# Handing out the next weights' four parts one product at a time, and queueing their VectorE work behind the last addition, in a Winograd-style TensorE trunk

## The chip, the cores and the metric

The kernel runs on one core of a Trainium2 chip. The metric is the device time of one launch in microseconds; three runs of the kernel before gave a median of 2574.48 us (2574.34 to 2576.41).

## The reference

The reference is one layer of a streaming encoder on 2048 tokens of width 1024, in float32. Cut to what matters here:

```python
h = rmsnorm(x, norm_mix_w)
u_b, u_c, u_h, z, xbc, dt_raw = jnp.split(h @ w_in, SPLITS, axis=-1)      # 1024 -> 5648
y_a = u_b * causal_dwconv(u_c * u_h, short_conv_w)                        # group A
y_b = ssd_mixer(z, xbc, dt_raw, ...)                                      # group B: chunked scan
x = x + concat([y_a, y_b]) @ w_out                                        # 2048 -> 1024
h = rmsnorm(x, norm_mlp_w)
x = x + square(relu(h @ w_up)) @ w_down                                   # 1024 -> 4096 -> 1024
return rmsnorm(x, final_norm_w)
```

So the work is four large products (w_in, w_out, w_up, w_down) with a state-space scan between the first two.

## The kernel before

**Products.** Every float32 operand is cut into a rounded part `hi` and the remainder `lo`, and a product is three matmuls: hi·hi, hi·lo, lo·hi (lines 300 to 302). Most products also go through a seven-product scheme for 2x2 blocks (class `Seven`): instead of eight block products, seven are made from sums of the blocks, called `b11 t1 t2 b21 t3 b22 t4`, in this order. One run of the seven is a **chain**; `chain` (line 273) writes it. A product of a chain is 12 matmuls of 128x512 (6 in one short chain). There are 113 chains: 20 and 22 for w_in (first and second half of the tokens), 8 for the first half of w_out ("outs"), 16 and 16 for w_up, 31 for w_down ("down"). The second half of w_out is made by plain products (`Output.unit`), between 1134 and 1328 us.

**Accumulators.** A chain uses three PSUM tiles, x, y and w. `b11`, `t2`, `t3` and `t4` all accumulate on x: x is read after t2, again after t3, and again after t4, and TensorE may not go on writing into it before the reader is done. So t4 needs the reader of t3, which has the time of one product (b22) for it, and t3 needs the reader of t2, with b21 between. `t1` and `b22` accumulate on y, `b21` on w.

**Evictions.** After each product `evict` reads the accumulator. In the w_in chains (`Proj.pair`, line 897) and the w_up chains (`Mlp.pair`, line 1143) t1 and t2 are copied by ScalarE, and t3 and b22 are added by VectorE (`add`, lines 928 and 1152). In the outs chains (`out_pair`, line 990, addition in line 1005) and the down chains (`Mlp.down`, line 1310, addition in line 1353) VectorE adds after all of the last six products.

**Weights.** The next chain's weights come as two raw tiles r0 and r1 (tag `wraw`, three buffers), loaded on SyncE's queue. `combine` (line 255) makes four parts of them, and each part is cut into `whi` (ScalarE, line 113) and `wlo` (VectorE, line 114), four buffers each:

```python
yield split_w(r0, nc.vector)                      # part 1, for b11 and b21
... s12 = r1a + r1b (L260);  s12b = s12a - r0a    # part 2, for t1 and t2
yield split_w(s12, nc.vector)
... s34a = r0a - r1a;  s34b = r0b - s12b          # part 3, for t3 and b22
yield split_w(s34, nc.vector)
yield split_w(r1[:, b], nc.vector)                # part 4, for t4
```

Here a and b are the two halves of a tile; `sub` is line 237, so L237 is any subtraction of this kind, on weights or on other blocks. Where the second half of the tokens meets the same w_in columns again, and in the later down chains, s12 and s34 are read back from DRAM (stored by lines 263 and 269), and VectorE has only the `wlo` part. The sums were computed 80 times.

**What sets the order.** The program is traced in this order: seven products, after each the evictions, then the parts that are handed out there (lines 314 to 318), then `after(name)`, which carries the side work (loading and cutting of the next blocks, the scan, the norms). A scheduler then fixes one queue for each engine. It takes an instruction as soon as it believes its inputs and buffers are ready; the order of the trace only decides between instructions that are ready together. So the sums of a later chain's weights can stand in VectorE's queue well ahead of an addition of an earlier chain. The queues themselves are strictly in order at run time: an instruction that waits holds up all that stand behind it. `behind(ins)` (line 108) adds an edge without a semaphore: whatever instruction in the block runs on the engine of `ins` is queued behind `ins`. Instructions on other engines are not touched by it.

In `chain`, `self.evicted` is the last ScalarE copy of t1 or t2 in a `Proj.pair`; in `Mlp` it is never set and the edge is empty. `self.added` is set in line 1353 alone, and used in `finish_first` (line 1497).

Of the kernel before, what the change touches and what calls it, by code (L numbers as in the profile page):

```python
# [14 lines left out]
ALU = mybir.AluOpType  # L15
# [24 lines left out]
def trunk(ctx: ExitStack, tc: tile.TileContext, x, x_tok, w_in, w_dt, w_out, w_up, w_down, cvec, hrow, out):  # L40
    nc = tc.nc
# [44 lines left out]
        out=tri, in_=tri, compare_op=ALU.is_ge, fill=0.0, base=0, pattern=[[1, P]], channel_multiplier=-1  # L86
# [21 lines left out]
    def behind(before):  # L108
        return tc.issue_after(before) if before is not None else nullcontext()
# [22 lines left out]
    def take(it, n=None):  # L132

        return list(itertools.islice((w for w in it if w is not None), n))
# [6 lines left out]
    def psum(tag, name, bufs=1):  # L141
        if tag in turns:
            tag, bufs = next(turns[tag])
        return ps.tile([P, 512], F32, tag=tag, name=name, bufs=bufs)

    class Rstd:


        def __init__(self, pool, tmp, n, w):
            self.pool, self.tmp, self.scale, self.w, self.n = pool, tmp, 1.0 / n, w, w // P  # L150
# [66 lines left out]
    class Seven:  # L217
        def __init__(self):
            self.places = [{} for _ in range(4)]
            self.unsettled = self.evicted = None  # L220
            self.amid = None

        def raw(self, name):
# [49 lines left out]
        def chain(self, groups, ws, ahead, evict, after):  # L273

            n = sum(len(g) for g in groups)
            pm = [{} for _ in groups]
            got = []
            PRODUCTS = (
                ("b11", 0, 0, "x", 1),
                ("t1", 1, 0, "y", 1),  # L280
                ("t2", 1, 1, "x", 0),
                ("b21", 0, 1, "w", 0),
                ("t3", 2, 0, "x", 0),
                ("b22", 2, 1, "y", 0),
                ("t4", 3, 0, "x", 0),
            )
            for name, wn, half, acc, first in PRODUCTS:
                at = half * n
                for gi, g in enumerate(groups):
                    if first:  # L290
                        pm[gi][acc] = psum("mm", "p" + acc, accs["mm"])
                    p = pm[gi][acc]
                    i, j = WHERE[name]
                    for k, place in enumerate(g):
                        if k == 2 and self.amid is not None:
                            self.amid()
                        hi, lo = (t[:, (at + k) * P : (at + k + 1) * P] for t in ws[wn])
                        h = [t[:, j] for t in place[i]]
                        kw = dict(skip_group_check=not first)
                        nc.tensor.matmul(p, hi, h[0], start=bool(first and k == 0), stop=False, **kw)  # L300
                        nc.tensor.matmul(p, hi, h[1], start=False, stop=False, **kw)  # L301
                        nc.tensor.matmul(p, lo, h[0], start=False, stop=(k == len(g) - 1), **kw)  # L302
                    at += len(g)
                for gi in range(len(groups)):
                    if name == "b11":

                        pm[gi]["w"] = psum("mw", "pw", accs["mw"])
                        self.copied = nc.scalar.copy(pm[gi]["w"], pm[gi]["x"]).ins  # L308
                    else:
                        evict(name, gi, pm[gi])  # L310
                if name == "b11" and self.unsettled:
                    self.settle(*self.unsettled, self.copied)
                    self.unsettled = None
                if ahead is not None:
                    if name == "t1":
                        next(ahead)
                    with behind(self.evicted):
                        got += take(ahead, {"b21": 2, "b22": 1, "t4": 1}.get(name, 0))
                after(name)
            return got  # L320

# [146 lines left out]
    class Proj(Seven):  # L468
# [428 lines left out]
        def pair(self, h, what, ws, ahead, after):  # L897
# [15 lines left out]
            else:  # L913
                a, b = self.e("ea"), self.e("eb")
            offb = 2 if kind == "ch" else off
            to = {
                "c11": a[:, off : off + TB],
                "c12": a[:, off + TB : off + TH],
                "c21": b[:, offb : offb + TB],
                "c22": b[:, offb + TB : offb + TH],  # L920
            }
            s = {}
# [3 lines left out]
                self.evicted = nc.scalar.copy(s[name], pm).ins  # L926

            def add(o, pm, name):
                nc.vector.tensor_tensor(out=to[o], in0=pm, in1=s[name], op=ALU.add)

            def evict(name, gi, pm):
                if name == "t1":
# [3 lines left out]
                elif name == "b21":  # L936
# [4 lines left out]
                    else:  # L941
                        nc.scalar.copy(to["c11"], pm["w"])
                elif name == "t3":
                    add("c22", pm["x"], "s5")
                    if kind == "z":
                        silu(to["c22"], to["c22"])
                    elif kind == "b":
                        mul(to["c22"], to["c22"], self.cc[n + 4][:, hi])
                elif name == "b22":
                    add("c12", pm["y"], "s2")  # L950
                    if kind == "z":
                        silu(to["c12"], to["c12"])
# [37 lines left out]
        def out_pair(self, n, ws, ahead, after):  # L990
            b0, b1 = (self.res.pop((n, b)) for b in range(NBB))
            lo, hi = slice(0, TB), slice(TB, TH)
            to = {"c11": (b0[:, lo], 0, 0), "c21": (b0[:, hi], 0, 1), "c12": (b1[:, lo], 1, 0), "c22": (b1[:, hi], 1, 1)}

            def evict(name, gi, pm):
                c, p, fin = {
                    "t1": ("c22", "y", 0),
                    "t2": ("c12", "x", 0),
                    "b21": ("c11", "w", 1),
                    "t3": ("c22", "x", 1),  # L1000
                    "b22": ("c12", "y", 1),
                    "t4": ("c21", "x", 1),
                }[name]
                t, b, i = to[c]
                nc.vector.tensor_tensor(out=t, in0=pm[p], in1=t, op=ALU.add)
                if fin:
                    nc.sync.dma_start(x1_d[n // 4 * NBB + b][:, 2 * (n % 4) + i], t)

            return self.chain([self.places], ws, ahead, evict, after)
# [115 lines left out]
    class Mlp(Seven):  # L1125
# [17 lines left out]
        def pair(self, h, q, ws, ahead, after):  # L1143

            e0, e1, e2 = (self.wide(n) for n in ("e0", "e1", "e2"))
            s = {}

            def copy(pm, name):
                s[name] = self.tmp(name)
                nc.scalar.copy(s[name], pm)  # L1150

            def add(o, pm, name):
                nc.vector.tensor_tensor(out=o, in0=pm, in1=s[name], op=ALU.add)

            def relu2(o, i):
                nc.scalar.activation(o, i, AF.Relu)
                nc.scalar.activation(o, o, AF.Square)

            def evict(name, gi, pm):
                if name == "t1":  # L1160
                    copy(pm["y"], "s5")
                elif name == "t2":
                    copy(pm["x"], "s2")
                elif name == "b21":
                    relu2(e0[:, 0], pm["w"])
                elif name == "t3":
                    add(e2[:, 1], pm["x"], "s5")
                    relu2(e2[:, 1], e2[:, 1])
                elif name == "b22":
                    add(e0[:, 1], pm["y"], "s2")  # L1170
                    relu2(e0[:, 1], e0[:, 1])
                else:
                    relu2(e1[:, 1], pm["x"])

            got = self.chain([self.places], ws, ahead, evict, after)
            self.unstored = h, q, e0, e1, e2
            return got
# [738 lines left out]
    with ExitStack() as c1:  # L1916
# [56 lines left out]
        for n in range(16, 32):  # L1973
# [4 lines left out]
            if n == 30:  # L1978
                ahead = mlp.weights(mlp.load_cols(w_up, (0, 1)))
# [78 lines left out]
```

## Time and profile before

| | |
|---|---|
| median of 3 runs | 2574.48 us (2574.34 to 2576.41) |
| the profiled execution's own time | 2574.36 us |
| its span, first to last instruction | 2572.5 us |
| TensorE matmul busy | 2556.2 us (99%), 11940 matmuls |
| VectorE busy | 1934.1 us (75%) |
| ScalarE busy | 1392.1 us (54%) |
| DMA | 546.44 MB, mean 212 GB/s |

All numbers of a profile come from one execution. Between the span and its own time lie 1.86 us outside the first and last instruction. A matmul's recorded end is modelled and overlaps the next one's start, so a stall of TensorE is read in two ways: as the idle time given in brackets before an instruction, and as the distance of two starts.

### The profile page before, as it was taken

How to read it: one execution, taken by the hardware profiler on the slowest of the kernel's cores; microseconds unless marked ns; L12 is line 12 of the kernel's file. 1: busy time of each engine (PE TensorE's matmuls, PEld its weight loads, DVE VectorE, ACT ScalarE, POOL GpSimd, SP SyncE). 2: the span in 40 equal slices, each digit the busy share in tenths (PEclk: the TensorE clock that was granted, in tenths of full speed). 3: DMA queues.
4: the chain of work that ended last, by engine and by line, in shares of the span. 5: the costliest groups of instructions: out<-in, count | busy, mean ns of one | idle time of the engine just before them, and what ended most of it. 6: DMA issues, size and time to landing. Idle time of an engine off the chain costs nothing.

```text
span 2572.5 us, 33309 instructions
## 1 busy us (share of the span) xinstructions
PE 2556.2 (99%) x11940; PEld 2103.7 (82%) x11940; DVE 1934.1 (75%) x2611; ACT 1392.1 (54%) x2158; POOL 69.4 (3%) x97
## 2 busy tenths in 40 slices
PE   9999999999999999999999999999999999999999
PEld 7887888888888887888888888888888888888887
DVE  7787686778887889978866865755559877876875
ACT  6553345876567865555345555655556444444443
POOL 1011000000000100000000000000000000000001
PEclk9999999999999999999999999999999999999999
DMA  6666455656556678878755764644358766676872
GB/s 232 225 215 243 155 166 192 200 188 205 187 176 193 188 238 284 301 256 266 246 186 200 277 219 160 243 161 154 139 176 273 256 200 208 222 241 216 280 253 78
DMA packets 266165, 546.44 MB, mean 212 GB/s; under 512 B 24848, under 2 KB 108432, under 8 KB 266000
## 3 DMA queue, kind: packets, MB, share of 16 engines
q1 hardware_dynamic: 265568, 543.92, 62.9%
q8 instruction: 94, 1.54, 0.2%
q14 instruction: 71, 0.58, 0.1%
q10 hardware_dynamic: 432, 0.39, 0.0%
HBM read 361.25 MB, written 182.98 MB: 212 GB/s over the span
## 4 chain that ended last, share of the span: by engine, by line
PE 91%; DMA 3%; ACT 2%; DVE 2%; issue 1%; SPq 0%; DVEq 0%; ACTq 0%
PE px L300 15%; PE px L301 15%; PE px L302 15%; PE py L300 7%; PE py L301 7%; PE py L302 7%; PE pw L300 4%; PE pw L302 4%; PE pw L301 4%; PE pm L137 3%; PE pm L139 3%; PE pm L138 3%; PE pm L524 1%; DMA ul<-y_d 1%; PE yd L1678 1%; DMA wraw<-w_down 1%
## 5 line engine op out<-in xcount | busy, mean ns | idle before, releaser
L300 PE MATMUL px<-uh,whi 128*128 128x512 f32 x1800 | 705.3, 392 | 5.0 <-DVE acc L1353 2.2
L301 PE MATMUL px<-ul,whi 128*128 128x512 f32 x1800 | 700.9, 389 | 0.8 <-DVE ul L369 0.6
L302 PE MATMUL px<-uh,wlo 128*128 128x512 f32 x1800 | 700.7, 390 | 0.0
L300 PEld LDWEIGHTS px<-uh,whi 128*128 128x128 f32 x1800 | 338.0, 188 | 81.0 <-DVE acc L1353 5.0
L302 PEld LDWEIGHTS px<-uh,wlo 128*128 128x128 f32 x1800 | 337.9, 188 | 71.4 <-DVE wlo L114 0.5
L301 PEld LDWEIGHTS px<-ul,whi 128*128 128x128 f32 x1800 | 338.0, 188 | 70.1 <-DVE ul L369 1.6
L113 ACT CAST whi<-s 128x1024 fp32r<-128x1024 f32 (+1 forms) x222 | 232.5, 1047 | 288.8 <-PE py L301 146.4
L114 DVE TENSOR_TENSOR wlo<-wraw,whi 128x1024 fp32r<-128x1024 f32 (+1 forms) x224 | 222.3, 992 | 182.6 <-ACT whi L113 182.2
L300 PE MATMUL py<-uh,whi 128*128 128x512 f32 x900 | 355.5, 395 | 0.0
L301 PE MATMUL py<-ul,whi 128*128 128x512 f32 x900 | 351.1, 390 | 0.0
L302 PE MATMUL py<-uh,wlo 128*128 128x512 f32 x900 | 351.0, 390 | 0.0
L114 DVE TENSOR_TENSOR wlo<-s,whi 128x1024 fp32r<-128x1024 f32 (+1 forms) x222 | 269.9, 1216 | 73.3 <-ACT whi L113 72.3
L113 ACT CAST whi<-wraw 128x1024 fp32r<-128x1024 f32 (+1 forms) x224 | 194.3, 867 | 235.4 <-PE px L301 169.7
L300 PEld LDWEIGHTS py<-uh,whi 128*128 128x128 f32 x900 | 169.0, 188 | 39.6 <-issue 4.8
L302 PEld LDWEIGHTS py<-uh,wlo 128*128 128x128 f32 x900 | 169.0, 188 | 35.4 <-issue 0.2
L301 PEld LDWEIGHTS py<-ul,whi 128*128 128x128 f32 x900 | 169.1, 188 | 33.9 <-issue 0.5
L356 DVE TENSOR_TENSOR ul<-rh,uh 128x1024 fp32r<-128x1024 f32 (+1 forms) x128 | 138.7, 1086 | 51.5 <-ACT uh L355 51.1
L300 PE MATMUL pw<-uh,whi 128*128 128x512 f32 x450 | 175.6, 390 | 0.0
L301 PE MATMUL pw<-ul,whi 128*128 128x512 f32 x450 | 175.2, 389 | 0.0
L302 PE MATMUL pw<-uh,wlo 128*128 128x512 f32 x450 | 175.1, 389 | 0.0
L355 ACT CAST uh<-rh 128x1024 fp32r<-128x1024 f32 (+1 forms) x128 | 119.9, 944 | 96.8 <-PE py L302 57.7
L308 ACT COPY pw<-px 128x512 f32<-128x512 f32 x118 | 67.6, 573 | 105.7 <-PE px L302 105.4
(266 smaller groups left out, 3612.9 us busy)
## 6 DMA issues: line engine op xcount, KB each, us to landing
hid_d<-e SPq DMA_DIRECT2D x96, 512.0 KB, 4.1
rh<-hid_d SPq DMA_DIRECT2D x96, 512.0 KB, 4.6
wraw<-w_in SPq DMA_DIRECT2D x67, 512.0 KB, 4.4
wraw<-w_up SPq DMA_DIRECT2D x62, 512.0 KB, 4.3
wraw<-w_down SPq DMA_DIRECT2D x88, 256.0 KB, 4.3
dec<-rd_d SPq DMA_DIRECT2D x32, 512.0 KB, 5.4
wraw<-w_out SPq DMA_DIRECT2D x32, 512.0 KB, 5.1
x<-x SPq DMA_DIRECT2D x24, 512.0 KB, 5.6
```

The costliest lines, as they stand in the source:

```text
L113: nc.scalar.copy(hi, raw)
L114: eng.tensor_tensor(out=lo, in0=raw, in1=hi.bitcast(F32), op=ALU.subtract)
L137: nc.tensor.matmul(out, whi, hi, start=(k == 0), stop=False)
L138: nc.tensor.matmul(out, whi, lo, start=False, stop=False)
L139: nc.tensor.matmul(out, wlo, hi, start=False, stop=(k == nk - 1))
L300: nc.tensor.matmul(p, hi, h[0], start=bool(first and k == 0), stop=False, **kw)
L301: nc.tensor.matmul(p, hi, h[1], start=False, stop=False, **kw)
L302: nc.tensor.matmul(p, lo, h[0], start=False, stop=(k == len(g) - 1), **kw)
L308: self.copied = nc.scalar.copy(pm[gi]["w"], pm[gi]["x"]).ins
L355: nc.scalar.copy(p[i][0], t)
L356: nc.vector.tensor_tensor(out=p[i][1], in0=t, in1=p[i][0].bitcast(F32), op=ALU.subtract)
L524: last[engine] = make(*args, **kw).ins
```

## The change

The four parts are handed out one each after b21, t3, b22 and t4, where before two came after b21 and one each after b22 and t4. And what a part issues on VectorE is queued behind the last addition that the evictions made (`self.added`), which three more lines now record.

```diff
     class Seven:
         def __init__(self):
             self.places = [{} for _ in range(4)]
-            self.unsettled = self.evicted = None
+            self.unsettled = self.evicted = self.added = None
             self.amid = None
...
                 if ahead is not None:
                     if name == "t1":
                         next(ahead)
-                    with behind(self.evicted):
-                        got += take(ahead, {"b21": 2, "b22": 1, "t4": 1}.get(name, 0))
+                    with behind(self.evicted), behind(self.added):
+                        got += take(ahead, name in ("b21", "t3", "b22", "t4"))
                 after(name)
...
             def add(o, pm, name):
-                nc.vector.tensor_tensor(out=to[o], in0=pm, in1=s[name], op=ALU.add)
+                self.added = nc.vector.tensor_tensor(out=to[o], in0=pm, in1=s[name], op=ALU.add).ins
...
                 t, b, i = to[c]
-                nc.vector.tensor_tensor(out=t, in0=pm[p], in1=t, op=ALU.add)
+                self.added = nc.vector.tensor_tensor(out=t, in0=pm[p], in1=t, op=ALU.add).ins
...
             def add(o, pm, name):
-                nc.vector.tensor_tensor(out=o, in0=pm, in1=s[name], op=ALU.add)
+                self.added = nc.vector.tensor_tensor(out=o, in0=pm, in1=s[name], op=ALU.add).ins
```

`name in (...)` is True or False and counts as one part or none. The three hunks at the end are lines 929 (`Proj.pair`), 1005 (`out_pair`) and 1153 (`Mlp.pair`); line 1353 set `self.added` already.

## Rows read from the trace of the kernel before

**Rows 1.** The page: busy time of each engine.
```profile
PE 2556.2 (99%) x11940; PEld 2103.7 (82%) x11940; DVE 1934.1 (75%) x2611; ACT 1392.1 (54%) x2158; POOL 69.4 (3%) x97
```

**Rows 2.** Stretches (outs, w_up, down): us; PE, PEld, DVE, ACT, POOL busy; clock; DMA.
```profile
955.00:1134.00 179.00, 175.85 (x878) 143.30 (x877) 158.62 (x226) 102.87 (x178) 0.00 (x0) 1.00 0.80 272
1653.00:1977.00 324.00, 324.00 (x1431) 268.39 (x1430) 200.17 (x264) 178.27 (x266) 0.00 (x0) 1.00 0.51 179
1977.00:2525.00 548.00, 545.73 (x2400) 449.52 (x2400) 423.67 (x528) 239.26 (x277) 0.00 (x0) 1.00 0.69 228
```

**Rows 3.** Waits of TensorE's matmuls, whole span: us in total, times, longest.
```profile
PE px L300 <- DVE acc L1353: 2.2, 4, 0.9
PE pss L1713 <- DVE ssq L1707: 1.9, 3, 0.7
PE px L300 <- ACT uh L368: 1.2, 1, 1.2
PE px L300 <- DVE x L1005: 1.2, 2, 0.8
```

**Rows 4.** Timeline (start, us), TensorE, a down chain: b22's last matmul, t4's first.
```profile
2041.10 0.39 PE L302 MATMUL py<-uh,wlo 128*128 128x512 f32 x1
2042.38 0.50 PE L300 MATMUL px<-uh,whi 128*128 128x512 f32 x1 [0.89 <-DVE acc L1353]
```

**Rows 5.** Timeline of VectorE, same chain; L1353 px is t3's addition.
```profile
2037.38 1.22 DVE L114 TENSOR_TENSOR wlo<-s,whi 128x1024 fp32r<-128x1024 f32 x1
2041.03 0.69 DVE L260 TENSOR_TENSOR s<-wraw 128x512 f32<-128x512 f32 x1 [2.44 <-DMA wraw<-w_down]
2041.64 0.68 DVE L1353 TENSOR_TENSOR acc<-px,acc 128x512 f32<-128x512 f32 x1
2042.24 0.68 DVE L237 TENSOR_TENSOR s<-s,wraw 128x512 f32<-128x512 f32 x1
```

**Rows 6.** Timeline of SyncE's queue, same chain: when the late load was issued.
```profile
2035.75 0.81 SPq L1227 DMA_DIRECT2D wraw<-w_down  x2
```

**Rows 7.** Timeline of VectorE at the other three such places.
```profile
2061.11 0.69 DVE L260 TENSOR_TENSOR s<-wraw 128x512 f32<-128x512 f32 x1 [2.55 <-DMA wraw<-w_down]
...
2118.82 0.69 DVE L260 TENSOR_TENSOR s<-wraw 128x512 f32<-128x512 f32 x1 [2.11 <-DMA wraw<-w_down]
...
2176.68 0.69 DVE L260 TENSOR_TENSOR s<-wraw 128x512 f32<-128x512 f32 x1 [2.14 <-DMA wraw<-w_down]
```

**Rows 8.** Timeline, an outs chain; L1005 px is t3's addition, the matmul t4's first.
```profile
1039.67 1.21 DVE L114 TENSOR_TENSOR wlo<-s,whi 128x1024 fp32r<-128x1024 f32 x1
...
1041.93 0.68 DVE L1005 TENSOR_TENSOR x<-px,x 128x512 f32<-128x512 f32 x1
...
1042.67 0.50 PE L300 MATMUL px<-uh,whi 128*128 128x512 f32 x1 [0.33 <-DVE x L1005]
```

**Rows 9.** Timeline of VectorE, just ahead of the other addition L1005 waited for.
```profile
974.71 1.89 DVE L369 TENSOR_TENSOR ul<-ul,uh 128x512 fp32r<-128x512 f32 x3
```

**Rows 10.** ScalarE by line and shape, 1977 to 2525 us: count, busy, mean ns, idle.
```profile
L113 ACT CAST whi<-s 128x1024 fp32r<-128x1024 f32 x56 | 59.0, 1053 | 35.1 <-PE py L301 15.6 <-PE pw L301 14.3 <-DVE s L237 2.2
```

**Rows 11.** Timeline, outs: part 2's wlo of the next chain, t1's first use of it.
```profile
982.50 1.23 DVE L114 TENSOR_TENSOR wlo<-s,whi 128x1024 fp32r<-128x1024 f32 x1
...
984.51 0.40 PE L302 MATMUL py<-uh,wlo 128*128 128x512 f32 x1
```

**Rows 12.** Timeline at one of the scan's waits.
```profile
821.78 1.22 DVE L114 TENSOR_TENSOR wlo<-s,whi 128x1024 fp32r<-128x1024 f32 x1
...
824.27 0.35 PE L1713 MATMUL pss<-ssq,ones_r 128*128 128x128 f32 x1 [0.72 <-DVE ssq L1707]
```

**Rows 13.** Timeline, a w_up chain: a load of r1, t3's addition, the load's sum.
```profile
1453.72 0.33 SPq L105 DMA_DIRECT2D wraw<-w_up  x1
...
1457.05 0.69 DVE L1153 TENSOR_TENSOR e<-px,s 128x512 f32<-128x512 f32 x1 [0.63 <-PE px L302]
1458.44 0.69 DVE L260 TENSOR_TENSOR s<-wraw 128x512 f32<-128x512 f32 x1 [0.71 <-DMA wraw<-w_up]
```

## The prediction

> **What bounds the kernel now.** I read the page's busy line first [rows 1]: TensorE's matmuls cover 99% of the span, while VectorE has 75% and ScalarE 54%. A matmul's end is modelled, so I took the busy time by stretch next [rows 2], to see what a full TensorE looks like. From 1653 to 1977 us it is never idle and starts 1431 matmuls in 324.00 us, one every 0.226 us, at clock 1.00. So 12 matmuls, one product of a chain, take 2.72 us, and a chain of seven 19.0 us. The down stage has 548.00 − 545.73 = 2.3 us without a matmul, the outs 179.00 − 175.85 = 3.2 us. That is about all that a better order can win there: the kernel runs at TensorE's pace, and this change removes no matmul. The third view, TensorE's waits [rows 3], names what can go: 2.2 us for the addition of line 1353 and 1.2 us for that of line 1005. The other two lines, the scan's ssq and the cut of fresh blocks in line 368, are touched only indirectly.
>
> The timeline then says why the additions are late. In a down chain b22 issues its last matmul at 2041.10, and t4's first comes at 2042.38 [rows 4]. In between, VectorE runs L260, the first sum of part 2, then t3's addition, then the next sum [rows 5]. L260 had sat 2.44 us at the head of the queue, waiting for a load of raw weights, and the addition behind it had been ready since about 2038.6, when t3's product ended (one product, 2.72 us, ahead of b22's end). The load it stood behind was issued at 2035.75 and used at 2041.03 [rows 5, 6]. These are not the weights of the next chain, whose part 2 gets its wlo at 2037.38, but of the one after it: the scheduler expected the load earlier and placed the sum a chain ahead of its place in the program's trace. The same pattern, with 2.55, 2.11 and 2.14 us at L260, stands three more times [rows 7], and those are the four waits for L1353.
>
> **The change part by part.** It adds and removes no instruction and no transfer. It moves four things.
>
> *Part 2 goes from b21 to t3, and its VectorE work behind t3's addition.* L260 of those four places goes behind the addition of the following chain, 19 us later, when its load has long landed, and the sum that is now due in this chain stands behind this chain's addition. So no sum stands ahead of it. t3's addition starts when its product ends and takes 0.68 us, and t4 has 2.72 us of b22 as cover. So the wait goes. Its worth is more than the idle time: from 2041.10 to 2042.38 are 1.28 us where 0.226 would do, so 1.05 us is lost for 0.89 us idle, 0.16 more. For four waits that is 2.2 [rows 3] + 4 x 0.16 = 2.84 us. In the outs, t4 waited 0.33 us for t3's addition at 1041.93, and part 2's wlo, 1.21 us, stood ahead of it [rows 8]. With it behind, the addition comes 1.1 us sooner, which ends this wait too: 0.33 + 0.16 = 0.49 us. The other wait for L1005, 0.8 us, I leave as it is: ahead of that addition stand three cuts of fresh blocks, 1.89 us [rows 9], and no weights. Sum: −3.33 us.
>
> *What part 2 loses.* From t3's end its chain is: addition 0.68, L260 0.69, L237 0.68 [rows 5], whi on ScalarE 1.05 [rows 10], wlo 1.23 [rows 11], together 4.3 us. t1 of the next chain uses wlo after b22, t4 and b11 (8.15 us) and two matmuls (0.45), so 4.3 us are left for other work in VectorE's queue. Below, this costs nothing, since nothing in it can speed TensorE up; above, it costs 2.72 us in a chain, if part 2 comes one whole product later than before where it had nothing to spare. The nearest row is the outs chain where 0.78 us was to spare (982.50 + 1.23 to 984.51 [rows 11]). There the sum stood behind t3's addition already, so I take nothing, and keep 2.72 − 0.78 = 1.9 us for the range.
>
> *Parts 1, 3 and 4.* Part 1's wlo is queued behind b21's own addition in outs and down, one instruction of 0.68 us. It is needed by b11, three products (8.15 us) later: nothing. In w_in and w_up the last addition at b21 is that of the chain before, so the edge binds nothing. Parts 3 and 4 wait for the additions of b22 and t4, but t3 and t4 of the next chain use them five and six products later: nothing. What is queued behind a waiting addition on VectorE is the side work and the scan; both ends of its cost are with the rivals. ScalarE's instructions get no new edge, but part 2's whi now waits for the later sums, and what stands behind it waits too: the last evictions of the chain and cuts of blocks, none of which TensorE needs before part 2 itself, in the next chain. Nothing again.
>
> *Transfers.* r0's buffer is held until s34b, and that is now behind b22's addition. In w_up the next r1 is issued at 1453.72 and its sum runs at 1458.44, 4.7 us later [rows 13]. After the change r0 comes free about 2.72 + 0.68 + 2 x 0.68 = 4.8 us after t3's addition started at 1457.05, at 1461.8, so the load lands near 1466.5. Its sum is not due until behind the next chain's t3 addition, at 1457.05 + 19.0 + 0.7 = 1476.8. The cover is 10 us. On SyncE's queue the stores of s12 and s34 (lines 263 and 269) come later with their sums and may hold the loads behind them; those feed blocks and weights due a product or more later. I cost both at nothing; if the cover were gone, one late block costs what the row of line 368 shows, 1.2 us [rows 3].
>
> So the profiled execution's 2574.36 us less 3.33 gives **2571.0 us**. That execution lies 0.12 us below the median of 2574.48, so it needs no shift: −0.13%.
>
> **The rivals.** *Buffers, not order (0.20).* The late sums come from a load that waits for one of three raw buffers: the four waits at L260 are alike, 2.1 to 2.6 us, and the load is issued only 5.3 us ahead [rows 5 to 7]. The change adds no buffer and holds r0's longer. If the additions are held up again, by the cut of other blocks or by b22-side sums, the gain is gone: 2574.4 us, no change. Against it: t3's addition needs no buffer of that load, only its place in the queue. The Trainium skill (Perfetto Trace Analysis, section Optimization Strategy) says that the same gap repeated on an engine can mean that there is no room for the next tile to be allocated, so that buffer counts or tile sizes are what to look at. By that rule alone the gap would outlive a change of order; the four alike waits fit it, but no row shows the addition itself short of a buffer.
>
> *More than the additions (0.17).* In the scan stage TensorE waits three times, 1.9 us, for ssq [rows 3], and at 824.27 a weights' wlo of 1.22 us stands in VectorE's queue shortly ahead of it [rows 12]. If the parts, spread out, no longer bunch there, 1.9 + 3 x 0.16 = 2.4 us go as well: 2571.0 − 2.4 = 2568.6. Against it: the scan's work is placed by the scheduler, and nothing ties it to the additions.
>
> *Part 2 late at t1 (0.12).* This is the case on the other side. In the outs VectorE is busy 158.62 of 179.00 us, 89% [rows 2], so the 4.3 us to spare shrink to little, and every instruction that the scheduler now puts between t3's addition and part 2's wlo counts. Each chain in which it comes a product later with only 0.78 us in hand waits 1.9 us; eight outs chains make 15.5 us: 2586.5. It decides the sign from 3.3 us of such waits on, and makes the kernel slower by over 0.2% from 8.5 us on, 1.06 us in each of eight chains. Against it: VectorE is at 77% in down (423.67 of 548.00) and 62% in w_up (200.17 of 324.00), so there it has room.
>
> **How the numbers follow.** 0.2% of 2574.48 is 5.15 us, about what a measurement of this kernel can tell from no change. My forecast has 0.51; around it I allow 0.05 beyond −5.15 us, if small waits go too, and 0.02 beyond +5.15. Faster: 0.05 + 0.17 = 0.22. Slower: 0.12 + 0.02 = 0.14. The same: 0.64. The range starts at 2567.6, a microsecond under the second rival, takes in the forecast and the first rival, and ends at 2577.5, which holds the forecast with three waits of 1.9 us lost; beyond lie most of the third rival and a thin tail below.
>
> **What would show it.** Right: L260 stands behind t3's addition in every down chain, no matmul waits for L1353, DMA waits of L260 shrink or go since the loads land a chain ahead, and part 2's wlo still ends before t1. TensorE's busy time by stretch changes by 2 to 3 us in down and 0.5 us in the outs, elsewhere not at all. Wrong: matmuls that wait for wlo (L114) at t1, new waits of pss for ssq, or t3's additions held up by other work.

## The result and the profile after

The changed kernel takes 2590.47 us (median of 6 runs, 2586.17 to 2594.23) against 2574.93 us (6 runs beside it): a ratio of 1.0059, 95% interval 1.0049 to 1.0069. It is slower by 15.5 us, 0.6%, where 2571.0 us had been forecast. The profiled execution took 2591.25 us with a span of 2589.5.

Page of the changed kernel, busy line:

```profile
PE 2563.8 (99%) x11940; PEld 2105.1 (81%) x11940; DVE 1927.0 (74%) x2611; ACT 1385.3 (53%) x2154; POOL 73.5 (3%) x97
```

Against [rows 1], VectorE and ScalarE are busy for 7 us less and TensorE's modelled busy time is up by 8. VectorE and TensorE have the same instructions and ScalarE four table loads fewer (the loads of tables for its activations); they stand in another order. The next two fences are stretches (us; PE, PEld, DVE, ACT, POOL busy; clock; DMA). The first is of the kernel before, for the second half of w_in beside the scan. The second is of the changed kernel: the same chains, from the start of the first to the start of the outs, then two stretches as long as those of [rows 2] for the outs and down, begun 15 and 16 us later:

```profile
452.00:955.00 503.00, 500.76 (x2598) 411.98 (x2597) 403.76 (x565) 352.66 (x654) 20.07 (x39) 1.00 0.62 196
```

```profile
452.40:966.10 513.70, 507.04 (x2599) 414.13 (x2598) 399.12 (x564) 347.26 (x649) 22.19 (x38) 1.00 0.61 192
970.00:1149.00 179.00, 174.19 (x867) 141.46 (x867) 157.40 (x226) 100.92 (x176) 0.00 (x0) 1.00 0.80 268
1993.00:2541.00 548.00, 545.58 (x2400) 449.78 (x2400) 426.83 (x533) 236.88 (x277) 0.00 (x0) 1.00 0.69 230
```

The same matmuls beside the scan, to within one, take 513.70 us instead of 503.00. The outs start 11 matmuls fewer in 179 us, and down as many as in [rows 2]. The clock is 1.00 in all of these. Laying the starts of the 113 chains (numbered from 0; chains 20 to 41 are those beside the scan) of the two traces side by side says the same: the changed kernel is 0.4 us late when the scan begins, 10.8 us when the outs begin, 15.1 at w_up, 16.9 at down and 16.7 at the end. Four chains of down come sooner, by 1.20, 1.03, 0.59 and 0.65 us: 3.47 together; others of down give as much back. What TensorE's matmuls now wait for (us in total, times, longest):

```profile
PE px L300 <- ACT pw L308: 6.0, 6, 1.5
PE px L300 <- DVE x L1005: 2.5, 4, 1.0
PE py L300 <- ACT s L1150: 1.7, 1, 1.7
PE st L138 <- DVE xde L1624: 1.5, 4, 0.6
...
PE px L300 <- DVE acc L1353: 0.8, 1, 0.8
PE yd L1678 <- DVE dec L1659: 0.8, 1, 0.8
...
PE py L302 <- DVE wlo L114: 0.4, 1, 0.4
```

Of [rows 3], the wait for ssq is gone, and L1353 falls from four waits to one, elsewhere. At the head is a ScalarE copy that had one wait of 0.3 us before, in w_up: L308 copies b11's accumulator, which t2 goes on writing. The place of [rows 4, 5] now looks as planned. VectorE, then TensorE, of the changed kernel:

```profile
2057.22 0.69 DVE L1353 TENSOR_TENSOR acc<-px,acc 128x512 f32<-128x512 f32 x1 [0.63 <-PE px L302]
2057.82 0.68 DVE L260 TENSOR_TENSOR s<-wraw 128x512 f32<-128x512 f32 x1
...
2059.51 0.39 PE L302 MATMUL py<-uh,wlo 128*128 128x512 f32 x1
2059.74 0.39 PE L300 MATMUL px<-uh,whi 128*128 128x512 f32 x1
```

The sum L260 stands behind t3's addition and waits for no load, and t4's first matmul follows 0.23 us behind b22's last. So the intended part works. The loss is somewhere else. Two of ScalarE's waits (whole span, changed kernel) that grew lead to it:

```profile
ACT whi L113 <- DVE s L237: 204.1, 76, 7.2
ACT dec L1653 <- DMA dec<-rd_d: 46.8, 24, 5.5
```

Before, they were 22.3 us in 9 waits and 25.3 us in 16. The first is the new edge seen from ScalarE. The second is the scan's: line 1653 is the relu on `dec`, eight instructions for a chunk, which wait for dec's load. dec has a single buffer, so the load is issued only when the matmuls `yd` of the chunk before have read it.

### The profile page after: what moved, and what is told of

It is laid out like the page before. It is cut to its first block, busy times and chain, and to the rows that moved or that the text cites. A ratio compares the mean times of both kernels' runs of the same rounds, so it can differ in the third digit from the quotient of the medians.

```text
span 2589.5 us, 33123 instructions
## 1 busy us (share of the span) xinstructions
PE 2563.8 (99%) x11940; PEld 2105.1 (81%) x11940; DVE 1927.0 (74%) x2611; ACT 1385.3 (53%) x2154; POOL 73.5 (3%) x97
## 4 chain that ended last, share of the span: by engine, by line
PE 57%; DMA 3%; DVE 3%; ACT 2%; issue 1%; SPq 0%; DVEq 0%; ACTq 0%
PE px L300 9%; PE px L301 9%; PE px L302 9%; PE py L300 5%; PE py L302 5%; PE py L301 5%; PE pm L138 2%; PE pm L137 2%; PE pm L139 2%; PE pw L300 2%; PE pw L301 2%; PE pw L302 2%; DMA ul<-y_d 1%; DMA dec<-rd_d 1%; DVE wlo L114 1%
## 5 line engine op out<-in xcount | busy, mean ns | idle before, releaser
L300 PEld LDWEIGHTS px<-uh,whi 128*128 128x128 f32 x1800 | 338.4, 188 | 88.0 <-ACT pw L308 10.5
L137 PE MATMUL pm<-uh,whi 128*128 128x512 f32 (+1 forms) x328 | 123.9, 378 | 0.0
```

Of the source, the lines that this page charges most:

```text
L137: nc.tensor.matmul(out, whi, hi, start=(k == 0), stop=False)
```

## The experiments

Most edits are in lines 317 and 318 of the changed kernel. Where an edit names P, the two lines read:

```python
with behind(self.evicted), behind(self.added if P else None):
    got += take(ahead, name in ("b21", "t3", "b22", "t4") if P else {"b21": 2, "b22": 1, "t4": 1}.get(name, 0))
```

so chains where P holds have the whole change and the others the order of before. "Late by" is always the start of a chain in the kernel's trace less that in the trace before. One trace against another differs by 1 to 2 us in stages that were not touched, so single steps under that size are not read as effects.

**Which half costs.** The handout alone, and the edge alone:

```diff
-                    with behind(self.evicted), behind(self.added):
+                    with behind(self.evicted):
```

> The parts go one each to b21, t3, b22 and t4 as in the change, but no VectorE work is queued behind an addition. Theory S (the handing-out costs it: part 2 now meets the two scan steps that are traced behind t3, and the scan stage is re-sorted): most of the 14 us that the changed kernel loses from 452 to 1134 us stays lost, so 2584 to 2590 us. Theory E (the edge costs it: VectorE's queue waits at an addition with weights and scan behind it): the scan stage is within 3 us of before, so 2572 to 2577 us. Without the edge the four waits for the addition of line 1353 may stay in the down stage.

```diff
-                        got += take(ahead, name in ("b21", "t3", "b22", "t4"))
+                        got += take(ahead, {"b21": 2, "b22": 1, "t4": 1}.get(name, 0))
```

> Two parts after b21, one each after b22 and t4 as before, with the edge behind the last addition. Theory S: the scan stage is as before within 3 us and the waits for line 1353 are gone, so 2570 to 2575 us. Theory E: the scan stage loses most of the 14 us, 2582 to 2588 us.

Measured: 2577.21 us, ratio 1.0002 [0.9993, 1.0012], and 2578.76 us, 1.0012 [1.0002, 1.0021]; before, 2575.74. Two of down's four waits go with the handout, all four with the edge. Beside the scan neither loses more than 0.8 us; with the edge alone VectorE and ScalarE run the instructions of chains 20 to 40 in the very order of before. The edge alone loses 4.8 us between the start of the outs and w_up, so it lies between the two theories. Neither half alone carries the 10 us beside the scan: that needs both together.

**Which stage costs.** The whole change in down alone, and everywhere but in the second half of w_in and the outs:

```diff
+P = hasattr(self, "dp")
```

> Both halves of the change in the down chains alone. In the changed kernel the down stage won 3.8 us at the four chains with late sums and lost 2.7 us at two other places. Both theories: scan stage exactly as before, 2571 to 2575 us. If it were above 2577, the loss would not come from the scan stage alone.

```diff
+P = getattr(self, "h", 0) != 1
```

> Both halves of the change everywhere but in the chains beside the scan (second half of w_in, and outs). Both theories: the 14 us of the scan stage come back, what is left is the 2 us lost in w_up and about 1 us won in down, 2572 to 2578 us. A third theory, that the loss is spread over all stages by later transfers, would leave it above 2582 us.

Measured: 2576.36 us, 1.0005 [0.9995, 1.0014], and 2578.07 us, 1.0008 [0.9999, 1.0017]; before, 2575.74. Nearly all of the loss is gone from both, so it is made beside the scan. But the gain isn't there either: down's four chains come 3.47 us sooner in both traces, and other chains of down give it back, one of them 1.84 and 2.30 us at chain 109. There the copy L308 stands behind a square of the final norm (L1496) on ScalarE that waits 5.11 and 5.55 us for its load. So I gave the change to fourteen chains of down, in whose steps of the program's trace the four late sums stand, and to no others:

```diff
+P = 6 <= getattr(self, "step", 0) < 20     # the chain's number in down
```

> The whole change in the down chains 6 to 19 of the stage alone, which hold the four late sums; the first chains of the stage and those beside the finished half's norm, where the down-only kernel gave back 3.5 us, stay as before. If the four waits are the change's whole worth and nothing is given back, 3.4 to 3.5 us faster than before, 0.13%. If the gain is given back wherever the change is made, no difference.

Measured: 2572.4 us, 0.9991 [0.9982, 1.0000]; before, 2575.19. This is the lowest median of the study, and all of the change's worth: the four chains come 3.48 us sooner in its trace, the medians lie 2.8 us apart, and the interval reaches 1.

**Which chains beside the scan.** The 22 chains of w_in alone, the eight outs alone, and everything but the edge at t3 in both:

```diff
+P = getattr(self, "beside", None) is True
```

> The whole change in the 22 w_in chains beside the scan alone; every other chain as before. In the changed kernel these chains lost 10.5 us, and neither half of the change alone lost there more than 1 us. Theory C (both halves together force part 2's wlo behind t3's addition, where the scan's two steps and the next evictions stand too): 10 us are lost again, 2583 to 2588 us. Theory D (the loss needs the other stages too, through the order that the scheduler carries on from them): under 4 us, 2574 to 2579 us.

```diff
+P = getattr(self, "beside", None) is False
```

> The whole change in the eight outs chains alone. The changed kernel lost 3.5 to 4 us there. Theory C: about that, 2577 to 2580 us. Theory D: the loss there is only the scan arriving late from the chains ahead, so nothing, 2574 to 2577 us.

```diff
-behind(self.added)
+behind(None if name == "t3" and getattr(self, "h", 0) == 1 else self.added)
```

> The whole change, but beside the scan (w_in's second half and outs) part 2's VectorE work, handed out after t3, is not queued behind the addition; the edges after b21, b22 and t4 stay. Theory C: the scan stage comes back to within 3 us of before, 2575 to 2580 us. Theory F (the edges at b22 and t4, or the spreading with any edge, make the loss): the 14 us stay, 2586 to 2592 us.

Measured, against 2575.19 us: 2588.1 us, 1.0058 [1.0041, 1.0074]; 2575.96 us, 1.0004 [0.9994, 1.0013]; 2583.02 us, 1.0031 [1.0020, 1.0043]. The w_in chains alone make the loss, 11.9 us by the start of the outs; the outs, where the forecast had looked for it, alone make none. Without the edge at t3 the outs begin 2.4 us late, not 10.8, so it is part 2's place that costs there; the rest of that kernel's loss, which puts it between its two theories, comes between the start of the outs and w_up (4.8 us). Then those 22 were divided, the six x chains (whose outputs go through a convolution on VectorE) from the others:

```diff
+P = getattr(self, "beside", None) is True and self.kind == "x"
```

> The whole change in the six x chains of w_in's second half alone (those whose evictions b22 and t4 each start a convolution of three VectorE instructions of 1.28 us). Theory G (behind t3's addition of an x chain VectorE is saturated until the middle of the next chain, so part 2's wlo, 1.22 us, moved from idle time ahead of the addition to behind it, makes the scan's work late, and TensorE waits for the scan in the chain after): 8 to 10 us lost, 2583 to 2586 us, all of it in the chains behind x chains. Theory U (every chain beside the scan loses alike, about 0.5 us): about 3 us, 2577 to 2579 us.

```diff
+P = getattr(self, "beside", None) is True and self.kind != "x"
```

> The whole change in the other 16 chains of w_in's second half alone (ch, b and z). Theory G: 0 to 3 us lost, 2575 to 2578 us. Theory U: about 8 us lost, 2582 to 2585 us.

Measured, against 2574.85 us: 2589.98 us, 1.0059 [1.0044, 1.0074], and 2577.52 us, 1.0011 [1.0001, 1.0021]. Six chains of 113 are enough for the whole loss, more than theory G had allowed; with the other sixteen the outs begin on time. The chains that grow most are those that follow an x chain. Chains 22, 27, 31, 35 and 37 last 24.0, 23.0, 23.0, 23.6 and 23.0 us before, 25.4, 25.1, 24.3, 26.6 and 24.4 in the changed kernel, and 25.2, 24.9, 25.5, 29.2 and 25.5 here.

**Is it VectorE's queue?** An x chain's successor has the convolution, the scan's step and the late part 2 on VectorE. I first moved work of the scan out of the way, tracing its second step behind b21 rather than t3 (in 21 of the w_in chains and in five of the outs, line 1109):

```diff
-                        for _ in range(1 + (name == "t3")):
+                        for _ in range(1 + (name == ("t3" if turn(m) or rest else "b21"))):
```

> The whole change everywhere, and in w_in's second half the second scan step that is traced behind t3 is traced behind b21 instead. Theory H (part 2 collides with the double scan step at t3): most of the scan stage's 14 us come back, 2577 to 2582 us. Theory G: the convolutions fill VectorE behind t3 whatever the place of the scan step, so the loss stays or grows, 2586 to 2600 us.

Measured: 2583.06 us, 1.0034 [1.0023, 1.0045]; before, 2574.85. Half comes back, between the two theories. It tells that the loss lies in how part 2 meets the scan's work, but not on which queue.

**Or ScalarE's?** Chains 34 (an x chain) and 35 show the meeting. Kernel before, VectorE and ScalarE; chain 35 starts at 796.09:

```profile
785.55 1.22 DVE L114 TENSOR_TENSOR wlo<-s,whi 128x1024 fp32r<-128x1024 f32 x1 [0.78 <-ACT whi L113]
787.42 0.69 DVE L929 TENSOR_TENSOR buf<-px,s 128x512 f32<-128x512 f32 x1 [0.65 <-PE px L302]
```

```profile
793.03 0.64 ACT L1704 ACTIVATE stmp<-y 128x512 f32<-128x512 f32 x1 [7.03 <-DVE y L1701]
793.58 0.38 ACT L1653 ACTIVATE dec<-dec,dd 128x128 f32<-128x128 f32 x1
793.90 1.24 ACT L879 ACTIVATE cacc<-buf,cv 128x1024 f32<-128x1024 f32 x1
...
799.11 0.57 ACT L308 COPY pw<-px 128x512 f32<-128x512 f32 x1
```

Part 2's wlo fills idle time ahead of t3's addition (L929 on px). The changed kernel, where chain 35 starts at 802.72, VectorE, ScalarE, and TensorE's wait:

```profile
794.05 0.69 DVE L929 TENSOR_TENSOR buf<-px,s 128x512 f32<-128x512 f32 x1 [1.49 <-PE px L302]
794.66 0.68 DVE L260 TENSOR_TENSOR s<-wraw 128x512 f32<-128x512 f32 x1
...
797.19 1.22 DVE L114 TENSOR_TENSOR wlo<-s,whi 128x1024 fp32r<-128x1024 f32 x1
...
802.40 1.29 DVE L881 SCALAR_TENSOR_TENSOR cacc<-buf,cv,cacc 128x1024 f32<-128x1024 f32 x1 [0.23 <-ACT cacc L879]
```

```profile
800.53 0.70 ACT L1653 ACTIVATE dec<-dec,dd 128x128 f32<-128x128 f32 x2 [3.38 <-DMA dec<-rd_d]
801.13 1.23 ACT L879 ACTIVATE cacc<-buf,cv 128x1024 f32<-128x1024 f32 x1
...
803.32 0.63 ACT L1704 ACTIVATE stmp<-y 128x512 f32<-128x512 f32 x1
...
807.60 1.28 ACT L130 ACT_TABLE_LOAD   x1
808.89 1.06 ACT L130 ACTIVATE cacc<-cacc 128x1024 f32<-128x1024 f32 x1
809.85 0.58 ACT L308 COPY pw<-px 128x512 f32<-128x512 f32 x1
```

```profile
810.49 0.50 PE L300 MATMUL px<-uh,whi 128*128 128x512 f32 x1 [1.53 <-ACT pw L308]
```

VectorE has idle time ahead of the addition that it can no longer use, and the scan's y (L1701) comes 1.2 us ahead of chain 35 instead of 3.8. In ScalarE's queue the relus of dec now stand ahead of the square of y (L1704) and ahead of the convolution's scale (L879). Before, the relus met a load that had landed while ScalarE waited for y; now they head the queue and wait 3.38 us for it, and the convolution, the splits of weights and the copy L308 stand behind. L308 ran 3.0 us into the chain before, 7.1 us now. The wait itself is only a part of that here: L879 starts 1.6 us ahead of the chain instead of 2.2. The rest is work that had stood behind L308: four more of the relus, and an activation with its table load (L130), 2.25 us from start to L308.

So the edge on VectorE was left as it is, and one on ScalarE was added: the relus queued behind the last convolution scale traced before them. In the kernel of the x chains, in the whole change, and as a control without the change beside the scan (but with it in down chains 6 to 19):

```diff
-            nc.scalar.activation(acc, buf[:, 0:TH], AF.Identity, ...)
+            Proj.conved = nc.scalar.activation(acc, buf[:, 0:TH], AF.Identity, ...).ins
...
-                relu = nc.scalar.activation(dec[:, i], ...)
+                with behind(Proj.conved): relu = nc.scalar.activation(dec[:, i], ...)
```

> The change in the six x chains alone, with one more edge: the scan's relus of dec (line 1653) are queued on ScalarE behind the last scale of a convolution (line 879) traced before them. Theory A (the loss is carried by ScalarE's queue, where a relu that waits for dec's load stands ahead of the convolution's scale): at least half of the 16 us of the kernel without this edge come back, 2575 to 2582 us, and the first line 881 of a convolution starts at its old place. Rival V (the loss is VectorE's own: part 2's wlo is moved out of idle time into a full stretch, and ScalarE's order only follows): less than a quarter comes back, 2586 us or more, with the scan's yd still 2 us or more later in the chains behind the x chains.

> The whole change with the same edge of the relus behind the convolution's scale. Theory A: some 5 us or more of the scan stage's 10 to 11 us come back, 2580 to 2585 us. Rival V: 2588 us or more.

> The handout of before in all of w_in and the outs, the whole change in down chains 6 to 19, and the relus behind the convolution's scale. It is the control for the kernel that has the edge and the change in the x chains, and a try for a faster kernel. Theory A (the edge gains nothing of itself, it only keeps the change from losing): the scan stage within 1.5 us of before, down 3 us shorter, 2571 to 2574 us. Rival W (the edge is worth some us of its own, which hid a loss in the x chains): the outs begin 3 us or more sooner than before, 2569 us or less.

Measured: 2576.29 us, 1.0005 [0.9995, 1.0014]; 2583.09 us, 1.0027 [1.0012, 1.0042], both against 2575.34; and 2572.93 us, 0.9995 [0.9986, 1.0004], against 2574.23. In the x chains the loss goes from 15.1 us to 1.0 (each against its own runs of before), and the outs begin 1.0 us late instead of 15.8; in the whole change it goes from 15.5 to 7.8. The control's scan stage equals that of before to 0.1 us, so the edge is worth nothing of itself and hid no loss. VectorE and ScalarE of the x kernel with the mended order, same place; chain 35 starts at 797.20:

```profile
788.53 0.69 DVE L929 TENSOR_TENSOR buf<-px,s 128x512 f32<-128x512 f32 x1 [2.66 <-PE px L302]
...
791.67 1.22 DVE L114 TENSOR_TENSOR wlo<-s,whi 128x1024 fp32r<-128x1024 f32 x1
...
796.56 1.28 DVE L881 SCALAR_TENSOR_TENSOR cacc<-buf,cv,cacc 128x1024 f32<-128x1024 f32 x1
```

```profile
795.01 1.24 ACT L879 ACTIVATE cacc<-buf,cv 128x1024 f32<-128x1024 f32 x1 [3.39 <-DVE buf L929]
...
801.10 0.57 ACT L308 COPY pw<-px 128x512 f32<-128x512 f32 x1
801.61 0.68 ACT L1653 ACTIVATE dec<-dec,dd 128x128 f32<-128x128 f32 x2
```

The wlo is behind the addition still, as late as in the changed kernel (3.1 us after it starts, in both), and the first L881 stands 0.6 us ahead of chain 35's start against 0.3. From the addition to that L881 VectorE's order is the same in the changed kernel, the x kernel and this one; behind it the second edge moved some of VectorE's work too. L308 is back at 3.9 us, and chain 35 lasts 23.4 us.

Two counts tell whether VectorE's order could be what was mended. From chain 20 to chain 40, 62 of the 542 instructions that VectorE had before are out of their old order in the x kernel, 63 with the mended relus, and 45 differ between these two (instructions outside the longest common sequence). So the time came back while VectorE's order did not. And in x chains 21, 26, 30 and 34 part 2's wlo starts 18.3, 14.8, 14.8 and 17.3 us into the chain with and without the mended relus (before: 14.2, 12.3, 12.3, 12.3), while the chains behind them last 23.5, 23.0, 23.0 and 23.4 us instead of 25.2, 24.9, 25.5 and 29.2. A late wlo alone therefore costs nothing there.

The group of relus from 452 to 970 us (busy us, mean ns | idle before), before, changed, x chains, and x chains with the mended order:

```profile
L1653 ACT ACTIVATE dec<-dec,dd 128x128 f32<-128x128 f32 x176 | 58.9, 392 | 15.9 <-DMA dec<-rd_d 15.2 <-DMA dd<-dt_d 0.7
```

```profile
L1653 ACT ACTIVATE dec<-dec,dd 128x128 f32<-128x128 f32 x176 | 59.4, 393 | 28.0 <-DMA dec<-rd_d 28.0
```

```profile
L1653 ACT ACTIVATE dec<-dec,dd 128x128 f32<-128x128 f32 x176 | 59.2, 393 | 30.0 <-DMA dec<-rd_d 29.9
```

```profile
L1653 ACT ACTIVATE dec<-dec,dd 128x128 f32<-128x128 f32 x176 | 57.8, 393 | 16.2 <-DMA dec<-rd_d 15.2 <-DMA dd<-dt_d 1.0
```

The idle time for dec's load goes from 15.2 us to 28.0 and 29.9, and back to 15.2. It is a sign and not the price: with the scan's step moved to b21 the same group sat idle 50.5 us for dec's load, and that kernel lost less. How much of the loss is the wait for the load, and how much the other work that moved with the relus, no run separates.

**The rest.** The change everywhere but in the x chains:

```diff
+P = not (getattr(self, "beside", None) is True and self.kind == "x")
```

> The change in every chain but the six x chains of the second half of w_in beside the scan. Theory X (the loss sits in the x chains): the 10 to 12 us of the scan stage come back almost whole, the outs keep some 4 us, down keeps its gain of about 3 us: 2575 to 2580 us, shift at the start of the outs below 3 us. Rival M (any chain beside the scan can lose it; the scheduler spreads the same lateness elsewhere): 2583 us or more, shift at the start of the outs above 6 us.

Measured: 2581.92 us, 1.0027 [1.0015, 1.0038]; before, 2575.34. The outs begin 3.5 us late, not 10.8, but w_up 9.7 us late: theory X missed the time by 2 us and the start of the outs by half a us, since the outs now lose 6 by w_up. This agrees with the whole change with mended order, 3.3 and 9.7 us. The largest single step there is the same kind of wait. ScalarE and TensorE of this kernel, in the outs:

```profile
1010.75 2.16 ACT L1653 ACTIVATE dec<-dec,dd 128x128 f32<-128x128 f32 x7 [7.31 <-DMA dec<-rd_d]
...
1014.80 0.58 ACT L308 COPY pw<-px 128x512 f32<-128x512 f32 x1
```

```profile
1015.43 0.50 PE L300 MATMUL px<-uh,whi 128*128 128x512 f32 x1 [2.48 <-ACT pw L308]
```

There is no convolution in the outs for the edge to hold the relus behind, and no run mended this place. That the outs' 4 to 6 us have this cause is read from the trace, not shown. The sixteen other chains of w_in alone, with the outs as before, already bring the same wait (9.45 us for dec at 1007.73, 1.67 us of TensorE for L308) and lose 4.1 us from the start of the outs to w_up; the outs alone lost nothing that can be told from no change. A second buffer for dec, which bears on the wait, wasn't tried. The 2.0 us that the changed kernel loses at the start of w_up's second half (the wait for L1150) were not followed up.

## Why the prediction was wrong

**The four waits: right, and a little more.** Step by step as worked out: L260 is behind t3's addition, its waits for w_down's loads are gone (19.9 us in 13 before, none in the list now), t4 follows b22. The sum was 2.84 us, the chains came 3.47 us sooner. The 0.16 us added to each bracketed wait was too small; 0.3 would have been right. The distance was taken to t4's first matmul alone, and in the trace before its second came 0.34 us behind that (2042.38 to 2042.72), where 0.226 would do. The first rival, buffers and not order, is ruled out for these four. But down as a whole gained only 0.1 us in the changed kernel: chains 86, 87 and 109 gave back 0.4, 1.1 and 1.6 us.

**The outs' 0.49 us: not seen.** L1005 now makes four waits, 2.5 us. In the chain of [rows 8] t4 still waits, 0.56 us at 1056.17: part 2's wlo is gone from in front of t3's addition, but two cuts of fresh blocks, idle 2.74 and 0.68 us before they start, and part 1's wlo of 1.21 us stand there instead. With the outs alone changed, no gain can be told from none.

**Parts 1, 3 and 4: here the step failed.** It said that ScalarE's instructions get no new edge, that what stands behind a later whi waits too, and "Nothing again". The step counted only what stands behind whi in today's order. The edge moves VectorE's sums and splits, and the scheduler then makes a new order for every queue. The relus of dec were nowhere in the working, although they are the one group beside the scan on ScalarE whose operand is a load with one buffer (23.2 us of waits in 15 places between 452 and 1140 us, with no wait of TensorE for L308 there). They came to the head of the queue and waited there, and their place is worth 14.2 of 15.1 us in the x chains, by the pair of runs with and without the mended order. In the whole change it is worth 7.8 of 15.5 us; the rest, most of it lost from the start of the outs on, has a cause read from the trace only.

**What part 2 loses: nothing, as taken.** TensorE hardly waits for wlo: one wait of 0.4 us. The third rival put 1.9 us into each of eight outs at t1, 2586.5 us. Its time is near what came, by accident: the outs alone cost nothing, and TensorE waits for L308, not for wlo. The text had named VectorE's busy share as the measure, 89% in the outs. Beside the scan it is 80% (403.76 of 503.00 us), but what set off the new order was that part 2 could no longer fill the idle time ahead of t3's addition in x chains; and with wlo just as late and the relus mended, the loss was gone.

**The range.** It left out a rival for the scan, where 22 chains change their order for no wait named there but ssq. The chance of 0.14 for the slower side came almost whole from waits that could be priced in the trace of before; a new order on a queue that the change doesn't touch was given none.

**Transfers: right.** Loads of raw weights do wait for s34b's subtraction now, up to 13.1 us (310.7 us in 32 waits of L105 on SyncE's queue, 3.1 us in 3 before), and TensorE's only listed wait for a part of the weights is the 0.4 us for wlo.

**The rule on repeated gaps.** By the Trainium skill (Perfetto Trace Analysis, section Optimization Strategy), alike gaps can mean that no room is left for the next tile. For the four gaps of [rows 5, 7] order alone ended them, in down chains 6 to 19 with all buffers as they were: the trace speaks against the rule there. The waits for dec do fit it, since dec's load is issued behind the matmul that frees its one buffer (21.8 us in 17 waits for yd on SyncE's queue, 452 to 970 us, changed kernel; 17.3 us in 15 before); no run gave it a second one.

**The second rival's observation** came true without its gain: the waits for ssq are gone from the list, and those for L308, xde and dec took their place.

## What to carry to other kernels

An edge on one queue is a new input for the scheduler of all queues: after such an edit compare the order of every engine, and look above all for an instruction that waits for a load and now stands ahead of others. Before an edge is set, ask in which stretches the moved work was filling idle time ahead of the instruction it is now put behind, for there the order will change; give the edge only to the chains whose waits it ends. Here 14 chains hold the whole gain of 3.5 us, and six chains with no gain are enough for a loss of 15.1.

## What the runs showed of the hardware

A wait in the trace costs TensorE more than its bracket: the four waits named 2.2 us in all, and without them the chains came 3.47 us sooner. Beside the scan the difference is larger: from 452 to 960 us the waits named grew from 2.2 to 6.1 us, while the chains there lost 10.5. So a list of TensorE's waits says where to look, and the starts of the chains say what it costs. Beyond that the loss came from the order of a queue and from what stood at its head.
